# One transformer block on one core: the late rows' norm and operands behind the up products of the third to sixth feed-forward groups, stored from the norm weight's tile

## The chip, the cores and the metric

The kernel runs on one core of a Trainium2 chip (trn2). The metric is device time in microseconds (us) of one execution, and the time of a kernel is the median over its runs. The five engines are named as in the profile: PE (TensorE), DVE (VectorE), ACT (ScalarE), POOL (GpSimd) and SP (SyncE, which here only issues DMAs). Each engine executes its instructions in a fixed order, which a scheduler writes down when the kernel is built. An instruction that has to wait therefore holds up everything behind it on its engine.

## The reference

One layer of width 1024 over 2048 rows (`S` = 2048, `D` = 1024, f32 in and out):

```python
u    = rms_norm(h, norm1_w[l])
proj = u @ w_in[l]                  # split into q, k, v of two kinds of heads
y    = concat(diff_attention(...), stick_breaking_attention(...))
h    = h + y @ w_out[l]
u2   = rms_norm(h, norm2_w[l])
gate = u2 @ w_gate[l]               # 1024 x 2816
up   = u2 @ w_up[l]                 # 1024 x 2816
h    = h + (silu(gate) * up) @ w_down[l]
```

The change lies in the last four lines, the feed-forward part.

## The kernel before

**Products.** Every f32 operand is held as two fp16 halves (high and low), and one product of two f32 blocks is three fp16 matmuls. The feed-forward products use one level of Strassen-Winograd: instead of eight block products, `quad` does seven, each 12 matmuls of 128x512 (`product`). For that, rows and weights are first mixed into seven operands; those of the rows are called X and lie in DRAM as `xcd[half]`.

**Steps.** The feed-forward part is 22 steps: two halves of 1024 rows, and in each half 11 groups of 256 columns (`NFG` = 11), `(half, fg)` in `steps`. A step is a gate quad (columns of `w_gate`), in some steps the down products of two groups that are finished (`down`, with 168 matmuls, in steps 2, 4, 6 and so on), and an up quad (columns of `w_up`). Counting from 0, step 2 works on the third group. Between the seven products of a quad stand hooks: `in_gate(1..7)` and `in_up(1..7)`; `row(s)` is called in each, with s = 1 to 7 in the gate quad and 8 to 14 in the up quad.

**Weights.** In the first half the hooks also drive `load_ffn` for the weights of the next group. For each of the three matrices a tile is fetched into one of two `stages` buffers (L925 for gate and up, L923 for down), ACT squares it into `sq`, which has one buffer (L954 for gate and up, L190 for down), PE forms the column sums `fsc` (L963), DVE makes scales of them (L964 and some small ones), and ACT and DVE write the scaled high and low halves (L216, L221) into the weight tile `wg`, `wu` or `wd`, while POOL mixes blocks (L98). The tile is also stored to `split` (L919), from where the second half reads it again. Three such chains follow one another in each step, since `sq` is one buffer, and PE executes the `fsc` matmuls in its fixed order.

**Quads.** The sums of the seven products are formed on DVE as they come: L1047, L1052, L1057, L1067, L1071. The tiles `cg` (gate) and `cu` (up) hold them; L1083 is the silu on ACT, L1103 the product of up and gate, L1097 and L98 make the fp16 operand `act` of the down products. PE writes the products into tiles of PSUM (`pa`, `pm`, `pd`), and a product that needs a used tile waits for DVE or ACT to have read it.

**Down.** `down` adds its products to the rows' residual: for each pair of row tiles, `load_hs` loads two tiles from DRAM (L1128) into the tag `hs`, which has four buffers, DVE adds (L1144), and the tiles are stored again (L1187). A load into a buffer waits until the store from it has landed.

**The late rows.** Rows 12 to 15 of the second half's 16 row tiles come too late from the attention part to be normed there. `build_x` does this for them in two pairs, j = 2 and 3. It takes all four `hs` buffers: `w2f` for the norm weight spread over 128 partitions, `xa` and `xb` for the pair's row tiles, and `xt`. It is a generator, and each call of `tick` runs it to its next `yield`: load (L1203), norm (`norm_tile`: ACT square L226, small scale L155, DVE product L229), 16 transposes on PE (L1213) with copies back on ACT (L1214), and then in `x_ops` four times `put`: a cast to fp16 on ACT (L89), a subtraction for the low half on POOL or DVE (L98), a store to `xcd[1]` (L238); between the puts stand four subtractions of operands (L98). The fp16 operands are formed in slices of `b16`, a tile with the tag `wd` used as three buffers. The operands are first read when the second half begins, in step 11 (`load_x(1, XL)`).

Where the ticks stand is in `late_at`: in steps 0 and 1, at the hooks listed there, and one tick ahead of step 0. The fetch of the second group's `w_up` is held until the second row tile's load is issued (`issue_after(rows[1].ins)`).

## Time and profile before

| | us |
|---|---|
| median of 3 runs | 2679.68 |
| lowest and highest run | 2678.3, 2680.41 |
| profiled execution, its own time | 2682.59 |
| span of the profiled execution | 2680.8 |
| PE busy in the span | 2492.4 (93%) |
| feed-forward steps 0 to 5 in the span | about 1427 to 1757 |

The profile records one execution. In a timeline a row gives the start, the busy time, the engine, the line, the operation with what it writes and reads, and how many instructions in a row it stands for; in square brackets stand the idle time of the engine just ahead, and what ended it. A row of several matmuls is pipelined: its busy time includes the tail of the last one, and the next row starts a little ahead of its end. In the steps considered here a product of 12 matmuls takes 2.75 us in a row of its own, and one follows the other every 2.59 us.

### The profile page before, as it was taken

To read this page: it belongs to the slowest core of one execution; us is meant where nothing else is said; L and a number is where in the kernel's file an instruction comes from. 1 tells how busy PE (TensorE), PEld (TensorE's weight loads), DVE (VectorE), ACT (ScalarE), POOL (GpSimd) and SP (SyncE) were. 2 spreads that over 40 slices of the span, in tenths; PEclk is the share of its full clock that TensorE was granted. 3 is DMA by queue.
4 is the path that set the end of the run, shared out by engine and by line. 5 is a ranking of instruction groups with operands and counts; after the bars stand their busy time and mean duration, and the time that the engine had idled before them with its cause. 6 is when DMAs were issued, how large, how long until landed. Compare 5 with 4: busy or idle time off the path is not lost. (4 is left out here: it accounts for less than half of the span.)

```text
span 2680.8 us, 50579 instructions
## 1 busy us (share of the span) xinstructions
PE 2492.4 (93%) x19628; PEld 1498.6 (56%) x19628; DVE 1932.7 (72%) x3711; ACT 1347.0 (50%) x2487; POOL 1489.1 (56%) x1098
## 2 busy tenths in 40 slices
PE   6998989888988989889989899999999999999999
PEld 4655656577776776557775344444444444444444
DVE  6898969898989989877766868777685544444434
ACT  4665656567978878665644535344352112111121
POOL 2578667667767766546764656565564232322323
PEclk9999999999999999999999899999999999999999
DMA  6777697767998979987897574665649743635532
GB/s 222 213 162 181 146 200 168 179 143 184 193 179 179 185 160 209 210 191 217 218 285 282 208 250 178 255 226 202 245 183 346 293 177 143 233 141 186 195 111 95
DMA packets 619585, 534.41 MB, mean 199 GB/s; under 512 B 480640, under 2 KB 548224, under 8 KB 609104
## 3 DMA queue, kind: packets, MB, share of 16 engines
q1 hardware_dynamic: 617520, 529.09, 69.9%
q8 instruction: 154, 2.52, 0.4%
q0 software_dynamic: 512, 1.36, 0.2%
q14 instruction: 87, 0.71, 0.1%
q10 hardware_dynamic: 1312, 0.72, 0.1%
HBM read 261.08 MB, written 147.32 MB: 152 GB/s over the span
## 5 line engine op out<-in xcount | busy, mean ns | idle before, releaser
L98 POOL TENSOR_TENSOR s<-z,s 128x1024 f16<-128x1024 f32 (+7 forms) x288 | 472.0, 1647 | 142.5 <-ACT s L89 109.8
L507 PE MATMUL sc<-kT,qT 128*128 128x512 f16 (+3 forms) x1520 | 382.0, 353 | 53.3 <-DVE z L623 19.3
L622 DVE TENSOR_TENSOR_SCAN z<-z,sc 128x512 f32<-128x512 f32 (+3 forms) x320 | 352.8, 1112 | 58.6 <-ACT sc L620 38.0
L1138 PE MATMUL pd<-wd,act 128*128 128x512 f16 x1764 | 390.9, 379 | 1.2 <-DVE cg L1071 1.2
L326 PE MATMUL pj<-w,xt 128*128 128x384 f16 x1920 | 352.2, 331 | 18.8 <-ACT xt L683 6.9
L1030 PEld LDWEIGHTS <-wg 128*128 128x128 f16 x1848 | 182.0, 99 | 230.2 <-issue 16.4
L518 PE MATMUL yp<-v,aT 128*128 128x64 f16 (+1 forms) x4896 | 269.8, 204 | 41.6 <-DMA aT<-s 40.2
L518 PEld LDWEIGHTS <-aT 128*128 128x128 f16 x4896 | 237.5, 99 | 120.4 <-DMA aT<-s 52.5
L1030 PEld LDWEIGHTS <-wu 128*128 128x128 f16 x1848 | 180.7, 98 | 218.0 <-issue 2.6
L98 POOL TENSOR_TENSOR act<-cg,act 128x512 f16<-128x512 f32 x112 | 148.5, 1337 | 262.9 <-ACT act L1097 150.8
L1138 PEld LDWEIGHTS <-act 128*128 128x128 f16 x1764 | 172.8, 98 | 209.4 <-issue 2.8
L326 PEld LDWEIGHTS <-xt 128*128 128x128 f16 x1920 | 187.3, 99 | 147.5 <-issue 21.4
L89 ACT CAST s<-z 128x128 f16<-128x128 f32 (+7 forms) x215 | 173.1, 809 | 134.1 <-DMA aT<-s 40.5
L98 POOL TENSOR_TENSOR hs<-hs,cu 128x512 f32<-128x512 f32 x99 | 130.9, 1328 | 171.3 <-DVE hs L1144 70.8
L619 ACT ACTIVATE z<-sc,c 128x512 f32<-128x512 f32 (+3 forms) x320 | 210.7, 663 | 25.6 <-PE sc L507 11.7
L1097 ACT CAST act<-cg 128x512 f16<-128x512 f32 x126 | 77.3, 616 | 238.4 <-DVE cg L1103 162.7
L507 PEld LDWEIGHTS <-qT 128*128 128x128 f16 x1520 | 128.4, 99 | 121.0 <-DVE z L623 23.0
L832 PE MATMUL po<-wo,mt 128*128 128x256 f16 x1536 | 180.7, 277 | 13.9 <-DVE xf L835 8.4
L1030 PE MATMUL pm<-X,wu 128*128 128x512 f16 x792 | 180.4, 379 | 1.3 <-DVE wu L221 1.3
L1030 PE MATMUL pm<-X,wg 128*128 128x512 f16 x792 | 181.3, 382 | 0.0
L342 PE MATMUL pj<-xt,w 128*128 128x128 f16 x2304 | 175.0, 220 | 6.7 <-DVE v L364 5.7
L1144 DVE SCALAR_TENSOR_TENSOR hs<-pd,c,hs 128x512 f32<-128x512 f32 x136 | 99.0, 747 | 109.6 <-PE pd L1138 83.1
(266 smaller groups left out, 4737.6 us busy)
## 6 DMA issues: line engine op xcount, KB each, us to landing
xt<-xs SPq DMA_DIRECT2D x112, 512.0 KB, 4.3
hs<-hd SPq DMA_DIRECT2D x68, 512.0 KB, 4.5
hd<-hs SPq DMA_DIRECT2D x56, 512.0 KB, 4.7
split<-wg SPq DMA_DIRECT2D x11, 1792.0 KB, 7.8
split<-wu SPq DMA_DIRECT2D x11, 1792.0 KB, 6.7
split<-wd SPq DMA_DIRECT2D x11, 1792.0 KB, 7.2
wg<-split SPq DMA_DIRECT2D x11, 1792.0 KB, 7.3
wd<-split SPq DMA_DIRECT2D x11, 1792.0 KB, 12.2
```

The source lines that it names most:

```text
L89: ACT.copy(dst, src)
L98: (DVE if e == "D" else POOL).tensor_tensor(dst, a_, b_, op)
L326: PE.matmul(pj[:, :384], lhsT=xv[:, xi, kt, :], rhs=G["w"][:, wi, kt, :], start=n == 0, stop=n == 23)
L342: PE.matmul(o, lhsT=x_ if c == 2 else w_, rhs=w_ if c == 2 else x_, start=n == 0, stop=n == 23)
L507: last = PE.matmul(sc[:, : 128 * w].rearrange("p (t n) -> p t n", n=P), lhsT=G["q"][i // 4][:, a_, i % 4, :], rhs=G["k"][q][:, b_, 0:w, :] ...
L518: PE.matmul(yp[:, y0 : y0 + wd], lhsT=aT[:, a_, :], rhs=v[:, v_ : v_ + wd], start=start and j == 0 and q == 0, stop=stop and j == nb - 1 a ...
L619: ACT.activation(om[:, lo:hi], sc[:, :w], AF.Sigmoid, scale=G["nkz"][:])
L622: DVE.tensor_tensor_scan(ov, ov, sc[:, :w], om[:, hi : hi + 1], op0=ALU.mult, op1=ALU.bypass)
L832: PE.matmul(po[:, sl], lhsT=mt[:, kt, P * xi : P * xi + P], rhs=wos[2 * h + n][wi][:, kt, :], start=q == 0, stop=q == 23)
L1030: front[0] = PE.matmul(ps_[:].rearrange("p (t n) -> p t n", n=P), lhsT=wv[:, wo, wi, 128 * kt : 128 * kt + 128], rhs=X[xo][:, :, xi, kt, : ...
L1138: front[0] = PE.matmul(po[:], lhsT=act[:, ao, xi, 128 * j : 128 * j + 128], rhs=W["d"][:, wo, wi, :], start=start and u == 0 and q == 0, s ...
L1144: DVE.scalar_tensor_tensor(dst, po[:], kd[:], src, op0=ALU.mult, op1=ALU.add)
```

## The change

Line numbers behind the first edits are lower by 2, later by up to 8; L1198 is the scaling of the norm weight (L1192 before), L1195 the row loads (L1203), L1196 the load of the norm weight (L1191), L1207 and L1208 the transposes and their copies (L1213, L1214).

- The ticks move from steps 0 and 1 to steps 2 and 3 (pair j = 2) and 4 and 5 (pair j = 3). In steps 2 and 4 they stand at hooks 9, 11, 12 and 13, all in the up quad, behind the down products; in steps 3 and 5 at hooks 7, 8, 9, 11 and 12.
- The four `hs` tiles are taken anew for each pair. The norm weight is loaded for each pair, behind the pair's two row tiles, and scaled for each pair.
- The fp16 operands are formed in the bytes of `w2f`, as one buffer in place of the three in `b16`. Each put's cast thus waits for the store of the put ahead.
- The norms of the two tiles stand in ticks of their own.
- The fetch of the second group's `w_up` isn't held any longer.

```diff
             def stage(fg, nme):
...
-                with tc.issue_after(rows[1].ins) if (fg, nme) == (1, "u") else nullcontext():
-                    fetch(st, f0, nme)
+                fetch(st, f0, nme)
...
             def build_x():
-                w2f, xa, xb, xt = (hp.tile([P, D], F32, tag="hs", bufs=4, name=nm("bx")) for _ in range(4))
-                SP.dma_start(w2f[:], a["norm2_w"].partition_broadcast(P))
-                DVE.tensor_scalar(w2f[:], w2f[:], r_24[:], None, op0=ALU.mult)
-                b16 = fd.tile([P, 7, 2, 512], F16, tag="wd", bufs=2, name=nm("b16"))[:].rearrange("p o s n -> p (o s n)")
-                n = [0]
-
                 def bufs():
-                    n[0] = (n[0] + 1) % 3
-                    return b16[:, 2048 * n[0] : 2048 * n[0] + 2048]
+                    return w2f[:].bitcast(F16)
 
                 d2 = lambda z: z[:].rearrange("p (d n) -> p d n", d=2)
                 for j in (2, 3):
+                    w2f, xa, xb, xt = (hp.tile([P, D], F32, tag="hs", bufs=4, name=nm("bx")) for _ in range(4))
                     for q, z in enumerate((xa, xb)):
-                        rows.append(SP.dma_start(z[:], hd[8 + 2 * j + q]))
+                        SP.dma_start(z[:], hd[8 + 2 * j + q])
+                    SP.dma_start(w2f[:], a["norm2_w"].partition_broadcast(P))
                     yield
+                    DVE.tensor_scalar(w2f[:], w2f[:], r_24[:], None, op0=ALU.mult)
                     for z in (xa, xb):
                         norm_tile(z[:], z[:], w2f[:], xt[:])
-                    yield
+                        yield
                     for z in (xa, xb):
...
                     yield from x_ops([d2(z) for z in (xa, xb)], d2(xt), 1, j, bufs, "AP", "DP")
+                    yield
...
-            tick(1)
             load_now(0, 0, "d", W)
...
-            late_at = ((5, 9, 10, 11, 12, 13, 14), (3, 7, 8, 9, 10, 11, 12))
+            late_at = {2: (9, 11, 12, 13), 3: (7, 8, 9, 11, 12), 4: (9, 11, 12, 13), 5: (7, 8, 9, 11, 12)}
...
-                    if i < 2 and s in late_at[i]:
+                    if s in late_at.get(i, ()):
                         tick(1)
```

What this does to the engines' orders is seen at three places. The first is DVE in the up quad of step 2. The rows of before: the last additions of the down products, the three sums of the up quad, and the maximum that belongs to the down weight's scale.

```order
L1144 SCALAR_TENSOR_TENSOR hs_23436<-pd_23548,c_23099,hs_23436 128x512
L1144 SCALAR_TENSOR_TENSOR hs_23435<-pd_23527,c_23099,hs_23435 128x512
L1047 TENSOR_TENSOR cu_23575<-pm_23579,cu_23575 128x512
L1052 TENSOR_TENSOR cu_23614<-pm_23601,cu_23575 128x512
L1057 TENSOR_TENSOR cu_23637<-pd_23624,cu_23614 128x512
L184 TENSOR_REDUCE m_23644<-fsc_23643 128x1
```

The same place of the change; `bx_23486` is `w2f`, `bx_23487` and `bx_23488` are `xa` and `xb`, and `xrs` is the small scale of a row's norm.

```order
L1142 SCALAR_TENSOR_TENSOR hs_23320<-pd_23412,c_22984,hs_23320 128x512
L1045 TENSOR_TENSOR cu_23460<-pm_23464,cu_23460 128x512
L155 TENSOR_SCALAR xrs_23548<-xss_23546 128x1
L1198 TENSOR_SCALAR bx_23486<-bx_23486,c_17372 128x1024
L1050 TENSOR_TENSOR cu_23506<-pm_23493,cu_23460 128x512
L155 TENSOR_SCALAR xrs_23575<-xss_23573 128x1
L229 SCALAR_TENSOR_TENSOR bx_23487<-bx_23487,xrs_23548,bx_23486 128x1024
L229 SCALAR_TENSOR_TENSOR bx_23488<-bx_23488,xrs_23575,bx_23486 128x1024
L1055 TENSOR_TENSOR cu_23529<-pd_23516,cu_23506 128x512
L184 TENSOR_REDUCE m_23536<-fsc_23535 128x1
```

The scaling of the norm weight and both norms now stand between the first and the third sum of the up quad; none of them was here before. On PE, the pair's 16 transposes (L1207) now stand in the same quad, between its sixth product (`pm_23579`) and its seventh, which adds to `pd_23516` after L1055 has read it.

The second place is SP behind the down products of step 2. Before, the stores of the rows (L1187) alternate with the loads for the next down (L1128):

```order
L1187 DMA hd<-hs_23365 128x1024
L1128 DMA hs_24071<-hd 128x1024
L1187 DMA hd<-hs_23364 128x1024
L1128 DMA hs_24072<-hd 128x1024
L1187 DMA hd<-hs_23436 128x1024
L1187 DMA hd<-hs_23435 128x1024
L1128 DMA hs_24235<-hd 128x1024
L1128 DMA hs_24236<-hd 128x1024
L925 DMA stages<-in_w_gate_dram 128x8x256
```

In the change the two row tiles and the norm weight take the places of these loads:

```order
L1185 DMA hd<-hs_23250 128x1024
L1195 DMA bx_23487<-hd 128x1024
L1185 DMA hd<-hs_23249 128x1024
L1195 DMA bx_23488<-hd 128x1024
L1185 DMA hd<-hs_23321 128x1024
L1185 DMA hd<-hs_23320 128x1024
L1196 DMA bx_23486<-in_norm_w_dram 128x1024
L923 DMA stages<-in_w_gate_dram 128x8x256
L917 DMA split<-wd_23534 128x7168
L238 DMA xcd_87<-bx_23486 128x2x1024 x2
L1126 DMA hs_24016<-hd 128x1024
L921 DMA stages<-in_w_down_dram 128x2x1024
```

The load of the norm weight is now the last one behind all the stores, ahead of the next `w_gate` fetch; the loads for the next down come behind the stores of the first operands.

The third place is ACT in step 3 of the change. L89 is the cast of a put, L216 and L952 belong to the weights of the next group (`sq_23788` is the square of the next `w_gate` tile).

```order
L89 CAST bx_23486<-bx_23488 128x2x512
L216 ACTIVATE wu_23693<-stages,c_23659 128x2x512 x2
L216 ACTIVATE wu_23693<-sx_23710,c_23659 128x512
L1081 ACTIVATE cg_23745<-cg_23745,c_23482 128x512
L1081 ACTIVATE cg_23762<-pa_23662,c_23482 128x512
L216 ACTIVATE wu_23693<-sq_23660,c_23659 128x2x512
L89 CAST bx_23486<-bx_23489 128x2x512
L952 ACTIVATE sq_23788<-stages 128x2048
```

The casts of the second and the third put, each of which writes into `w2f`, now stand ahead of the weights' work of this step; before, no cast of the late rows stood in step 3.

More of the change, by code (lines that the diff above doesn't have):

```diff
@@ L894, in block @@
             scales = {}
-            rows = []
             front = [None]
```

## The prediction

> **What bounds the kernel now.** First the page's line of busy times, then a table of stretches of 60 us, to see where in the feed-forward part PE is not full. Its columns are the stretch, its length, busy time (and count) of PE, PEld, DVE, ACT, POOL, the granted clock of PE, the DMA share and GB/s.
>
> ```profile
> PE 2492.4 (93%) x19628; PEld 1498.6 (56%) x19628; DVE 1932.7 (72%) x3711; ACT 1347.0 (50%) x2487; POOL 1489.1 (56%) x1098
> ...
> 1460.00:1520.00 60.00, 52.53 (x250) 25.11 (x249) 50.62 (x61) 32.21 (x42) 42.56 (x26) 0.94 0.61 226
> 1520.00:1580.00 60.00, 52.92 (x240) 24.19 (x238) 44.56 (x70) 26.00 (x31) 37.53 (x27) 0.94 0.68 237
> 1580.00:1640.00 60.00, 60.00 (x289) 28.40 (x288) 42.27 (x67) 26.74 (x32) 29.06 (x21) 1.00 0.63 223
> ...
> 1700.00:1760.00 60.00, 59.34 (x286) 27.89 (x284) 46.92 (x75) 31.88 (x38) 30.41 (x22) 1.00 0.59 214
> ```
>
> PE is the bound, but not everywhere. In steps 0 to 2, where the late rows are now (up to 1520) and just behind them, PE lacks 7 us in each stretch and its clock is 0.94. From step 2's up quad to step 3 (1580 to 1640) and in step 5 (1700 to 1760), where they are to go, PE is full at clock 1.00, with DVE at 42 to 47 us. So the change takes work from where PE waits and puts it where it doesn't.
>
> Next, PE's timeline: every gap of steps 0 to 2.
>
> ```profile
> 1443.88 2.76 PE L1030 MATMUL pd<-X,wg 128*128 128x512 f16 x12 [0.96 <-DMA X<-xcd]
> ...
> 1466.50 2.75 PE L1030 MATMUL pd<-X,wu 128*128 128x512 f16 x12 [1.36 <-DVE cu L1057]
> ...
> 1491.13 4.76 PE L1030 MATMUL pd<-X,wg 128*128 128x512 f16 x12 [5.47 <-DVE cg L1057]
> ...
> 1517.50 2.75 PE L1030 MATMUL pd<-X,wu 128*128 128x512 f16 x12 [0.64 <-DVE cu L1057]
> ...
> 1533.90 1.87 PE L963 MATMUL fsc<-sq,ones 128*128 128x256 bf16 x8 [5.88 <-ACT sq L954]
> 1535.56 7.34 PE L1030 MATMUL pm<-X,wg 128*128 128x512 f16 x24
> ...
> 1547.98 1.46 PE L1138 MATMUL pd<-wd,act 128*128 128x512 f16 x6 [1.19 <-DVE cg L1071]
> 1549.37 1.03 PE L963 MATMUL fsc<-sq,ones 128*128 128x256 bf16 x8
> ```
>
> The longest but one is DVE's doing. Its own rows ahead of L1057:
>
> ```profile
> 1484.25 2.17 DVE L229 SCALAR_TENSOR_TENSOR bx<-bx,xrs,bx 128x1024 f32<-128x1024 f32 x1
> 1486.34 3.48 DVE L221 SCALAR_TENSOR_TENSOR wu<-stages,c,wu 128x1024 f16<-128x1024 f32 x2
> ...
> 1490.40 0.68 DVE L1057 TENSOR_TENSOR cg<-pd,cg 128x512 f32<-128x512 f32 x1
> ```
>
> A norm of the late rows (2.17) and the weight split behind it hold L1057, and PE with it.
>
> **What leaves steps 0 to 2.** From 1443 to 1534 the stalls are 0.96 + 1.36 + 5.47 + 0.64 + 5.88 = 14.31 us. After the 5.47 the 12 matmuls took 4.76 for the usual 2.75: 2.01 more at a lowered clock, in all 16.3. I let all of it go. The 5.88 ends on the square of the next gate weight, which stands on ACT behind the down weight; that weight's tile has the tag of `b16`, whose stores are gone. The 1.19 and the slow clock behind the 5.88 (7.34 for 24 matmuls) I keep: between the two `fsc` rows at 1533.90 and 1549.37 lie 15.5 us, and that is a weight chain by itself. One undisturbed, in step 3:
>
> ```profile
> 1608.52 1.04 PE L963 MATMUL fsc<-sq,ones 128*128 128x256 bf16 x8
> ...
> 1623.86 1.04 PE L963 MATMUL fsc<-sq,ones 128*128 128x256 bf16 x8
> ```
>
> ```profile
> 1620.94 1.91 ACT L954 ACTIVATE sq<-stages 128x2048 bf16<-128x2048 f32 x1 [0.61 <-DVE wu L221]
> ```
>
> From the `fsc` to the end of the next square are 1622.85 − 1608.52 = 14.3 us, so two `fsc` can't follow much closer. That is also why a gap closed may come back: bounds of the gain are 16.3, and 5.5 if only the L1057 and L1057-like stalls of DVE (5.47) go and the rest is met again by the chain. I take 16.3, since step 3's chains, with no late rows beside them, leave PE no gap.
>
> At this place a rule can be weighed. The clock after the 5.47 gap was lowered (4.76 for 2.75). The Trainium skill, "TensorE: Matmul & The Clock Gate", Part 1: The HAM clock gate, has PE fall to half its clock after an idle window of about 3.4 us and come back after as long a busy one; by that rule a full window of 12 matmuls at half clock would cost an estimated 2.6 us, the trace's row says 2.0, and the sum goes by 2.0.
>
> **What moves without a price.** The late rows' work itself, from the view of that tile (min/median/max in ns, all counts of both pairs):
>
> ```profile
> L89 ACT CAST b<-bx x8: 618/1045/1069, 1456.2 to 1509.6; 128x1024 f16<-128x1024 f32 x6, 128x512 f16<-128x512 f32 x2
> ...
> L229 DVE SCALAR_TENSOR_TENSOR bx<-bx,xrs,bx x4: 1906/2160/2284, 1448.8 to 1491.0; 128x1024 f32<-128x1024 f32 x4
> L98 POOL TENSOR_TENSOR b<-bx,b x3: 2367/3108/3118, 1459.7 to 1512.4; 128x1024 f16<-128x1024 f32 x3
> L98 POOL TENSOR_TENSOR bx<-bx,bx x3: 2132/2157/2249, 1469.7 to 1507.4; 128x512 f32<-128x512 f32 x3
> ...
> L1192 DVE TENSOR_SCALAR bx<-bx,c x1: 752/752/752, 1445.3 to 1445.3; 128x1024 f32<-128x1024 f32 x1
> ```
>
> ```profile
> 1452.53 1.04 PE L1213 MATMUL xtr<-id,bx 128*128 128x128 f32 x8
> ```
>
> The transposes are on PE before and after: 1.04 us for eight, with a tail that the next row covers, so 2.05 for a pair's 16 at most. One more scaling (0.75) and one more load of 512 KB are added, whose places are below.
>
> **What it costs in steps 2 and 3.** SP's rows at the end of step 2's down:
>
> ```profile
> 1590.09 0.32 SPq L1128 DMA_DIRECT2D hs<-hd  x1
> 1590.50 0.86 SPq L1187 DMA_DIRECT2D hd<-hs  x2
> 1595.72 1.54 SPq L1128 DMA_DIRECT2D hs<-hd  x2
> ```
>
> ```profile
> hs<-hd SPq DMA_DIRECT2D x3, 512.0 KB, 4.4
> hd<-hs SPq DMA_DIRECT2D x2, 512.0 KB, 5.6
> ```
>
> Each load follows the landing of a store (the last two rows are the DMA issues from 1588 to 1597, with the median us to landing). The last load, at 1595.72, becomes the norm weight's. By the 4.4 it lands at 1600.1. The square of the first tile writes `xt`, in the buffer of the last store, and can't start ahead of 1596 either. On DVE, L155 and L1198 then wait directly behind the first sum of the up quad:
>
> ```profile
> 1589.36 0.69 DVE L1047 TENSOR_TENSOR cu<-pm,cu 128x512 f32<-128x512 f32 x1 [1.84 <-PE pm L1030]
> ```
>
> Queued behind them are the second and third sum, both norms and the down weight's maximum, and PE waits for these: its transposes need the norms, its seventh product the third sum.
>
> ```profile
> 1599.67 2.75 PE L1030 MATMUL pd<-X,wu 128*128 128x512 f16 x12
> ```
>
> So DVE stands from 1590 to 1600.1; then 0.75 + 0.69 + 2 x 2.16 make 1605.9. PE is at its transposes at 1599.67, does the first eight (1.04) behind the first norm, waits, and has done all at about 1607: 5.4 us of stall beside the 2.05 of transposes, and as after the 5.47 gap 2.0 of slow clock.
>
> Three more rows are needed: the page's landing of the operands' stores, the stretch at the start of step 3 (columns as above), and a DVE row in it.
>
> ```profile
> xcd<-b SPq DMA_DIRECT2D x6, 512.0 KB, 5.8
> ```
>
> ```profile
> 1595.00:1612.50 17.50, 17.50 (x87) 8.31 (x86) 17.01 (x27) 9.90 (x13) 8.46 (x6) 1.00 0.69 252
> ```
>
> ```profile
> 1605.91 1.75 DVE L1103 SCALAR_TENSOR_TENSOR cg<-cu,c,cg 128x512 f32<-128x512 f32 x1
> ```
>
> Behind that the puts run one at a time, as all four write into `w2f`: cast 1.05, subtraction 3.1, issue 0.4, landing (5.8) make 10.35 each. With the first cast at 1608.5, the third is at 1629.2; POOL's own operand subtractions (2.16 and 3.1) stand between, to about 1635.6. The square of the next gate weight stands behind that cast on ACT (1.91), so its `fsc`, at 1623.86 before, comes at 1637.6: 13.7, less the 2.05 that the transposes only move, is **11.7**. DVE has little room there (17.01 of 17.50 us are busy). Its rows are also stretched while POOL subtracts: L1103 took 1.75 us here, L1047 on the same size 0.69 above. Operand subtractions that fall to DVE and one or two such stretches of 1.0 I put at 1.8, an estimate: 13.5.
>
> At this stretch a second rule can be weighed. The Trainium skill, "SBUF — State Buffer", section SBUF: two separate sides, has VectorE and GpSimd share a pair of ports that one instruction locks for its whole length. That speaks against the change: a subtraction of 3.1 put beside a full DVE could hold it for its full length, not for 1.0, and by it each pair would lose an estimated 3 us more; the sum takes the 1.8.
>
> **What it costs in steps 4 and 5.** The same, with less wait for the loads:
>
> ```profile
> 1704.48 0.40 SPq L1187 DMA_DIRECT2D hd<-hs  x1
> 1705.78 6.97 SPq L1128 DMA_DIRECT2D hs<-hd  x2
> ```
>
> The second of the last two loads is issued behind 1712, so the store at 1704.48 landed 7.9 us after its issue; the square waits for it, and L155 starts at about 1713.6. From there stand on DVE L1198 and L1103 (0.75 each), the two norms (4.3), and between these the rest of the down weight's split and two sums (some 4 us, an estimate from the 3.48 + 0.68 of L221 and L1057 above): the second norm ends at 1723.6. PE would begin its transposes at 1714.98:
>
> ```profile
> 1714.98 2.75 PE L1030 MATMUL pa<-X,wg 128*128 128x512 f16 x12
> ...
> 1737.41 1.04 PE L963 MATMUL fsc<-sq,ones 128*128 128x256 bf16 x8
> ```
>
> That is 7.6 us, and 2.0 of slow clock. The `fsc` at 1737.41 comes at 1748.2: 10.8, less 2.05 for the transposes, is **8.7**; with the same stretch 10.5. The steps behind I let stand as they are.
>
> **The sum.** −16.3 + 11.7 + 8.7 = +4.1 without the stretch, −16.3 + 13.5 + 10.5 = +7.7 with it; I take the middle, +5.9. The profiled execution's own time is 2682.59 (1.8 around its span), 2.9 above the median of the runs; it becomes 2688.5, and the median 2679.7 + 5.9 = **2685.6**.
>
> **Rivals.** (1) Faster: DVE isn't held. That is so if the norm weight has landed and the first square is done when DVE gets to L1198 (by 1590 in the terms above), and if the chain of puts is hidden behind step 3's products. Price: the stalls and slow clocks (5.4 + 2.0 and 7.6 + 2.0) go, of each pair only its scaling and norms on a full DVE stay (0.75 + 2 x 2.16 = 5.1), the sum is −16.3 + 10.2 = −6.1, 2673.6. For it: the down loads before it land within 4.4. Against: the load waits for a store's landing, and the 1595.72 is in the trace. It decides from a load issued ahead of about 1586 (4.4 ahead of 1590). (2) The gain fails: the weight chain is the bound of steps 0 to 2, and only 5.5 go; −5.5 + 20.4 to 24.0 = +14.9 to +18.5, 2696.4 in the middle. For it: every second gap ends on that chain; against: step 3 has no gap. (3) The norm weight's load takes as long as the one in the trace:
>
> ```profile
> bx<-in_norm_w_dram SPq DMA_DIRECT2D x1, 512.0 KB, 10.0
> ```
>
> That is 5.6 more for pair one; for pair two 1705.8 + 10.0 = 1715.8 for the 1713.6 above, 2.2 more: 2693.4. Against: beside that load four others started. (4) Gains and losses meet, and nothing is measured, or the work stands in other places than the steps suppose: within 0.2%.
>
> **How the numbers follow.** Within 0.2% (5.4 us) is what a measurement of this kernel can hardly tell from no change. Forecast 0.42, of its own range 2680 to 2692, which lies on both sides of that bound: 0.27 slower, 0.15 same. Rival 1: 0.2, of it 0.18 faster. Rival 2: 0.13, rival 3: 0.15, both slower. Rival 4: 0.10. In sum slower 0.55, same 0.27, faster 0.18. The range reaches from rival 1 to rival 2 and a little over: 2672 to 2698; left out are the gain of 16.3 with no loss (2663) and rivals 2 and 3 together (2704).
>
> **What would show it.** In the profile after: no gap over 2 us on PE in steps 0 and 1, and the one on `sq` L954 in step 2 gone; then a gap of some 5 us ahead of L1207 in step 2's up quad and of 7 in step 4's, both ended by DVE `bx` L229, with DVE's own idle ended by the norm weight's DMA or `xrs`; and a gap ahead of L963 in steps 3 and 5 ended by ACT `sq` L952. The forecast is wrong if DVE's L1198 doesn't wait, or if L963 in steps 3 and 5 isn't late by about 10 us.

## The result, and the profile after

The changed kernel takes 2690.65 us (median of 5 runs, 2687.61 to 2695.94), the kernel before 2679.68 (5 runs, 2677.7 to 2684.17). The ratio is 1.0039, with a 95% interval of 1.0027 to 1.0052: slower by 10.5 us (7.2 to 13.9). The forecast was 2685.6, slower by 5.9.

The profiled execution has a span of 2694.1 us, 13.3 longer than before, and 3.2 of these lie ahead of the feed-forward part, where both kernels do the same work. In the profiled executions of this study the first gate product starts anywhere from 1417.9 to 1430.4 us. So traces are compared from that product on: 1253.58 us to the end of the span before, 1263.73 after, +10.15, which is what the runs say. The stretches of 60 us show where (columns as in the prediction; the start is 3.2 us later than before).

```profile
1460.00:1520.00 60.00, 60.00 (x293) 28.54 (x292) 47.82 (x69) 31.64 (x38) 36.97 (x27) 1.00 0.50 191
1520.00:1580.00 60.00, 56.42 (x266) 26.00 (x265) 34.53 (x51) 18.19 (x22) 32.02 (x24) 1.00 0.63 225
1580.00:1640.00 60.00, 49.98 (x233) 23.44 (x231) 52.22 (x83) 34.47 (x45) 36.24 (x23) 0.94 0.56 204
...
1700.00:1760.00 60.00, 51.51 (x234) 24.54 (x233) 45.40 (x66) 31.23 (x40) 30.75 (x19) 0.91 0.56 198
```

The picture of before is turned round: PE is full from 1460 to 1520 and lacks 8 to 10 us, at a lowered clock, in the two stretches that were full. PE's timeline of the changed kernel from the end of step 2 to step 5 has these gaps, shown with the later sums of each gate quad:

```profile
1584.51 1.09 PE L1207 MATMUL xtr<-id,bx 128*128 128x128 f32 x8 [2.72 <-DVE bx L229]
1586.34 1.06 PE L1207 MATMUL xtr<-id,bx 128*128 128x128 f32 x8 [0.73 <-DVE bx L229]
...
1598.39 1.03 PE L961 MATMUL fsc<-sq,ones 128*128 128x256 bf16 x8 [0.84 <-ACT sq L952]
...
1611.74 5.28 PE L1028 MATMUL pd<-X,wg 128*128 128x512 f16 x12 [4.34 <-DVE cg L1055]
...
1621.38 1.03 PE L961 MATMUL fsc<-sq,ones 128*128 128x256 bf16 x8 [1.39 <-ACT sq L952]
...
1718.33 1.97 PE L1207 MATMUL xtr<-id,bx 128*128 128x128 f32 x8 [3.99 <-DVE bx L229]
1720.09 4.43 PE L1028 MATMUL pa<-X,wg 128*128 128x512 f16 x12
...
1742.83 4.22 PE L1028 MATMUL pd<-X,wg 128*128 128x512 f16 x12 [3.21 <-DVE cg L1055]
...
1749.26 1.04 PE L961 MATMUL fsc<-sq,ones 128*128 128x256 bf16 x8
```

There are two kinds: at the transposes, which wait for the norms, and ahead of the fourth gate product, which waits for the third sum. After the longer ones the clock is low (5.28, 4.43 and 4.22 us for 12 matmuls that take 2.75). The first kind in DVE's timeline:

```profile
1571.32 0.69 DVE L1045 TENSOR_TENSOR cu<-pm,cu 128x512 f32<-128x512 f32 x1 [1.84 <-PE pm L1028]
1580.51 0.15 DVE L155 TENSOR_SCALAR xrs<-xss 128x1 f32<-128x1 f32 x1 [8.50 <-ACT bx L226]
1581.85 0.76 DVE L1198 TENSOR_SCALAR bx<-bx,c 128x1024 f32<-128x1024 f32 x1 [1.19 <-DMA bx<-in_norm_w_dram]
```

DVE stands for 8.50 us behind the first sum, as foreseen. The square on ACT ends this wait, and 1.19 more goes to the norm weight, which comes last. The square in turn waits for a store, the one from the buffer that `xt` takes over (ACT's timeline):

```profile
1579.33 1.06 ACT L226 ACTIVATE bx<-bx 128x1024 f32<-128x1024 f32 x1 [11.32 <-DMA hd<-hs]
```

The second kind is in DVE's timeline, in step 3's gate quad, ahead of the L1055 that PE waits for:

```profile
1596.60 2.17 DVE L98 TENSOR_TENSOR bx<-bx 128x512 f32<-128x512 f32 x1
1598.69 1.75 DVE L98 TENSOR_TENSOR act<-cg,act 128x512 f16<-128x512 f32 x1
1600.36 1.75 DVE L1101 SCALAR_TENSOR_TENSOR cg<-cu,c,cg 128x512 f32<-128x512 f32 x1
...
1609.44 1.65 DVE L98 TENSOR_TENSOR bx<-bx,bx 128x1024 f16<-128x1024 f32 x1
1611.01 0.68 DVE L1055 TENSOR_TENSOR cg<-pd,cg 128x512 f32<-128x512 f32 x1
```

Behind 1590.48 no row up to 1611.01 has idle time ahead of it. Late-row subtractions stand between the sums; those that DVE does ahead of 1611.01 take 5.2 us (2.17, 1.65 and two of 0.68). The kernel's own rows beside them take up to 1.75 (L1101 takes 0.74 to 0.75 a few rows earlier) while POOL mixes the next weight, as it did before (L1103 with 1.75 in the prediction):

```profile
1598.17 1.73 POOL L98 TENSOR_TENSOR sx<-stages 128x512 f32<-128x512 f32 x1
1599.97 1.59 POOL L98 TENSOR_TENSOR stages<-stages 128x512 f32<-128x512 f32 x1
```

The L1101 at 1600.36 ends at 1602.1, 0.55 behind the end of POOL's second row. The Trainium skill, "SBUF — State Buffer", section SBUF: two separate sides, has an instruction of VectorE with two inputs in SBUF and one of GpSimd that reads SBUF keep each other out, whichever starts first, until its end. By that rule L1101 begins its work at about 1601.6; the 0.55 that is left is 0.2 short of the 0.74 that it takes alone, so the trace agrees roughly.

In step 5 it is the kernel's own weight split that holds L1055, with a late-row subtraction on POOL beside it. DVE's rows, then POOL's:

```profile
1737.34 4.83 DVE L221 SCALAR_TENSOR_TENSOR wu<-stages,c,wu 128x1024 f16<-128x1024 f32 x2 [1.27 <-ACT wu L216]
1742.10 0.68 DVE L1055 TENSOR_TENSOR cg<-pd,cg 128x512 f32<-128x512 f32 x1
```

```profile
1737.98 3.11 POOL L98 TENSOR_TENSOR bx<-bx,bx 128x1024 f16<-128x1024 f32 x1
```

One such L221 took 1.27 at 1713.12; here two take 4.83.

**A ruler.** The column sums of the gate and up weights (`fsc<-sq`, eight matmuls, L963 before) stand at about the same places of the steps in every kernel and mark off what a stretch of PE's timeline lasts. Numbered from step 0, the fifth is at the start of step 2's down (1549.37 before), the sixth and seventh at the two ends of step 3's gate quad (1608.52, 1623.86), the ninth in step 4's down (1668.99), the tenth and eleventh in step 5 (1721.24, 1737.41), the thirteenth in step 6's down (1780.78). The table gives the distances between their starts in each kernel's profiled execution, beside the feed-forward part as a whole and the ratio of the runs. Where a stretch holds the same instructions in the same order it repeats to 0.1 us (101.0 and 59.2).

| kernel | feed-forward | to sum 5 | 5-6 | 6-7 | 7-9 | 9-10 | 10-11 | 11-13 | runs against before (95%) |
|---|---|---|---|---|---|---|---|---|---|
| before | 1253.6 | 122.2 | 59.2 | 15.3 | 45.1 | 52.3 | 16.2 | 43.4 | |
| change | 1263.7 | 101.0 | 67.1 | 23.0 | 44.7 | 62.6 | 20.6 | 44.9 | 1.0039 (1.0027 to 1.0052) |
| e1 no late rows | 1231.4 | 100.9 | 59.2 | 15.3 | 44.7 | 51.6 | 16.6 | 43.2 | 0.9912 (0.9897 to 0.9928) |
| e2 pair one | 1249.5 | 101.0 | 66.3 | 23.0 | 46.4 | 52.7 | 16.2 | 44.6 | 0.9973 (0.9962 to 0.9983) |
| e3 pair two | 1246.5 | 101.0 | 59.2 | 15.3 | 44.7 | 61.4 | 21.0 | 44.4 | 0.9962 (0.9949 to 0.9974) |
| e4 old place | 1258.3 | 125.7 | 60.5 | 15.3 | 45.1 | 52.2 | 16.2 | 43.4 | 1.0016 (1.0003 to 1.0028) |
| e5 POOL | 1269.7 | 101.0 | 65.5 | 25.9 | 48.9 | 59.5 | 23.6 | 45.5 | 1.0067 (1.0051 to 1.0082) |
| e6 halves | 1265.4 | 101.0 | 65.6 | 23.7 | 46.8 | 60.3 | 23.1 | 45.1 | 1.0044 (1.0028 to 1.0060) |
| e7 later norms | 1258.4 | 101.0 | 59.2 | 22.7 | 46.7 | 56.6 | 26.4 | 45.3 | 1.0015 (1.0004 to 1.0026) |
| e8 one each | 1252.7 | 112.8 | 59.2 | 22.3 | 46.2 | 52.4 | 16.6 | 43.2 | 0.9997 (0.9986 to 1.0008) |
| e9 no subtractions | 1248.3 | 100.9 | 68.8 | 14.8 | 44.7 | 61.9 | 13.8 | 43.4 | 0.9987 (0.9975 to 1.0000) |
| e10 steps 6, 7 | 1250.6 | 100.9 | 59.2 | 22.7 | 46.8 | 52.8 | 16.2 | 43.2 | 0.9988 (0.9975 to 1.0002) |
| e11 up quad | 1254.0 | 100.9 | 59.2 | 16.4 | 54.5 | 52.7 | 16.2 | 43.2 | 1.0007 (0.9998 to 1.0016) |
| e12 norms apart | 1259.8 | 101.0 | 62.2 | 21.4 | 48.2 | 51.8 | 16.2 | 43.4 | 1.0030 (1.0015 to 1.0045) |

The difference of the feed-forward column from before, and that of the runs (ratio times 2680), agree within 3.2 us in every row, so the table may be read as the time to that extent.

The scheduler doesn't always put a sum behind the same matmul, and then two neighbouring stretches trade matmuls of 0.216 us each (2.59 for 12). Between sums 5 and 6 the change has 275 of them for 269 before, and between 6 and 7 it has 61 for 67. So of the 7.9 us by which 5-6 grows, 1.3 come from 6-7. The next table takes these matmuls out, and the 2.05 of the pair's transposes where they stand; what is left is PE time lost against before.

| kernel | matmuls in 5-6 and 6-7 | lost in 5-6 | lost in 6-7 |
|---|---|---|---|
| before, e1 | 269, 67 | 0 | 0 |
| change | 275, 61 | 4.6 | 8.9 |
| e2 pair one | 275, 61 | 3.8 | 9.0 |
| e5 POOL | 275, 61 | 3.0 | 11.9 |
| e6 halves | 276, 60 | 2.9 | 9.9 |
| e7 later norms | 269, 67 | 0.0 | 5.4 |
| e9 no subtractions | 275, 61 | 6.3 | 0.8 |
| e12 norms apart | 283, 53 | 0.0 | 7.0 |

In the same way 9-10 has 242 matmuls in the change for 237 before, and 10-11 has 64 for 67: 7.2 us are lost ahead of step 5's gate quad and 5.1 in it.

### The profile page after: what moved, and what is told of

Read it like the earlier page. It is cut to its first block, busy times and chain, and to the rows that moved or that the text cites. A ratio compares the mean times of both kernels' runs of the same rounds, so it can differ in the third digit from the quotient of the medians.

```text
span 2694.1 us, 50591 instructions
## 1 busy us (share of the span) xinstructions
PE 2506.2 (93%) x19628; PEld 1504.2 (56%) x19628; DVE 1935.0 (72%) x3713; ACT 1346.8 (50%) x2488; POOL 1485.1 (55%) x1096
## 3 DMA queue, kind: packets, MB, share of 16 engines
q8 instruction: 154, 2.52, 0.4%
## 5 line engine op out<-in xcount | busy, mean ns | idle before, releaser
L326 PE MATMUL pj<-w,xt 128*128 128x384 f16 x1920 | 358.6, 335 | 14.7 <-ACT raw L375 5.8
L89 ACT CAST s<-z 128x128 f16<-128x128 f32 (+7 forms) x215 | 173.2, 810 | 137.9 <-DMA aT<-s 46.4
## 6 DMA issues: line engine op xcount, KB each, us to landing
wd<-split SPq DMA_DIRECT2D x11, 1792.0 KB, 11.7
```

The costliest lines, as they stand in the source:

```text
L89: ACT.copy(dst, src)
L326: PE.matmul(pj[:, :384], lhsT=xv[:, xi, kt, :], rhs=G["w"][:, wi, kt, :], start=n == 0, stop=n == 23)
```

## The experiments

### What a pair costs, in each place: e1 to e4

e1 leaves the late rows out: no tick runs, and the second half reads the first half's operands for pairs 2 and 3. e2 and e3 leave one pair out in the same way. The edit of e1:

```diff
-            late_at = {2: (9, 11, 12, 13), 3: (7, 8, 9, 11, 12), 4: (9, 11, 12, 13), 5: (7, 8, 9, 11, 12)}
+            late_at = {}
...
-                    SP.dma_start(X[o][:].rearrange("p t s k n -> p (t s k n)"), xcd[half][o].rearrange("p t n -> p (t n)"))
+                    for src, j0, j1 in (((1, 0, 2), (0, 2, 4)) if half else ((0, 0, 4),)):
+                        SP.dma_start(X[o][:, j0:j1].rearrange("p t s k n -> p (t s k n)"), xcd[src][o][:, j0:j1].rearrange("p t n -> p (t n)"))
```

> The late rows are left out altogether: no load, norm, transpose or operand of row tiles 12 to 15; the second half's first groups read the first half's operands in their place, over the same bytes. What is left is the steps without them, so that both kernels can be held against it. Theory 1 (place): before the change the late rows cost PE about 17 us of stalls and slow clock in steps 0 to 2 and 4.1 us of transposes; the time is about 2679.7 - 21 = 2659. Theory 2 (chain): the weights' chains bound steps 0 to 2 anyway, and without the late rows only 5.5 us of stalls and the 4.1 go: about 2670.

Measured: 0.9912, 23.6 us less than before. The part up to the fifth sum takes 100.9 us for 122.2, 21.2 less. Theory 1 holds: what the late rows cost there goes with them, 4.1 of transposes by the prediction's count and so 17.1 of waits and slow clock. The weights' chains bound these steps only between sums 4 and 5, where e1 keeps gaps of 1.96 and 1.61. The change gets all of the 21.2 (101.0).

> The changed kernel with pair j = 2 alone, in steps 2 and 3; pair j = 3 is left out, its operands are the first half's. Theory 1: pair one costs what the trace shows between the column sums of step 2 and of step 4, 12.6 us beside 2.05 us of transposes, so 14.7 above e1. If the two pairs' losses are independent, this and the next add up to the changed kernel. Theory 2 (a pair's cost comes from what both hold together, such as the second load of the norm weight or the row loads pushed back): clearly less than 14.7, and the sum of both falls short of the changed kernel by 5 us or more.

> The changed kernel with pair j = 3 alone, in steps 4 and 5; pair j = 2 is left out. Theory 1: 13.1 us between the column sums of step 4 and of step 5, 2.05 us of transposes and 1.5 us in step 6, so 15 to 17 above e1. Theory 2: clearly less, the rest only when both are there.

Measured: e2 lies 18.1 us above e1 in the feed-forward part, e3 15.1; by the runs 16.4 and 13.4. 18.1 + 15.1 = 33.2 for the 32.3 by which the change lies above e1, so by the traces the two pairs are independent. By the runs they add up to 29.8 for 34.0; that is 4.2 short, less than the 5 that theory 2 asked for, and each ratio is known only to some 3 us. Neither pair costs clearly less than theory 1 said, so theory 2 falls, though the runs alone wouldn't exclude a few us of it. Of e2's 18.1, 14.8 lie between sums 5 and 7, as in the change. Of the rest, 1.7 lie between 7 and 9 (24 matmuls take 6.77 for 5.34 behind a gap of 2.63 ahead of sum 7), 1.1 between 9 and 10, where five more matmuls stand than in e1, and 1.4 in step 6, where e2 has no late rows: there the product behind a gap of 3.31, which is 3.30 before, takes 5.28 for 4.13.

e4 puts the changed code back to the old place:

```diff
+            tick(1)
             load_now(0, 0, "d", W)
...
-            late_at = {2: (9, 11, 12, 13), 3: (7, 8, 9, 11, 12), 4: (9, 11, 12, 13), 5: (7, 8, 9, 11, 12)}
+            late_at = {0: (5, 6, 9, 10, 11, 12, 13, 14), 1: (1, 3, 4, 7, 8, 9, 10, 11, 12)}
```

> The changed code (norm weight loaded per pair, operands formed in its tile one at a time, norms in ticks of their own) at the ticks of before: steps 0 and 1. Theory 1 (place): the loss of the change is that of steps 2 to 5, so this is near the kernel before; the 5.9 us stall on the square in step 2 should go since no weight buffer is taken, the puts that wait for one another may give some of it back: 2672 to 2682. Theory 3 (form): the waits of the casts for the stores in one tile are what costs, and they cost here as well: 2685 to 2695.

Measured: 1.0016, +4.3 us; 1258.3 in the feed-forward part. That is between the two expectations. In the old place the form of the change, with the three more ticks that it needs, costs 4.7 us (1258.3 for 1253.6). The stall of 5.88 ahead of the fourth sum is gone, as theory 1 had it, but PE has others in its place: 4.97 ahead of transposes, 3.68 and 2.52 ahead of fourth gate products and 3.04 for a load of X, in all 17.8 us of gaps up to the fifth sum for 15.5 before. With the same code the pairs cost 26.9 us in steps 0 and 1 (1258.3 for e1's 1231.4) and 32.3 where they now are. So of the change's 10.2, 4.7 go with the form, as far as its price in the old place tells, and 5.4 with the place.

### The gate quad: puts or subtractions? e5, e6, e9

The prediction had the stretch behind the norms grow because puts wait for one another in one tile, so that ACT's square stands behind a cast. The rival is that DVE and POOL have no room for the subtractions. e5 moves all of them to POOL, e6 removes the wait between puts.

```diff
-                    yield from x_ops([d2(z) for z in (xa, xb)], d2(xt), 1, j, bufs, "AP", "DP")
+                    yield from x_ops([d2(z) for z in (xa, xb)], d2(xt), 1, j, bufs, "AP", "P")
```

> The changed kernel with all subtractions of the late rows on POOL (before, POOL or DVE by load). Theory 1 (DVE is full in the gate quad of steps 3 and 5): DVE gets 5.2 us of each pair back between its 1595 and 1612, L1055 comes earlier and PE's gaps of 4.34 and 3.21 ahead of the fourth gate product shrink to under 2, with their slow clock: 6 to 10 us less than the changed kernel, so 0 to +5 against before. Theory 2 (the puts wait for one another in one tile): each subtraction gets longer (2.6 to 3.1 on POOL for 1.65 on DVE), the third cast and the square behind it come later: +10 to +16 against before.

Measured: 1.0067, +18.0 us, beyond even theory 2's range and not for its reason. PE's gaps and POOL's and ACT's rows in step 3's gate quad:

```profile
1605.66 2.75 PE L1028 MATMUL pd<-X,wg 128*128 128x512 f16 x12 [2.11 <-DVE cg L1055]
...
1620.47 1.87 PE L961 MATMUL fsc<-sq,ones 128*128 128x256 bf16 x8 [9.47 <-ACT sq L952]
```

```profile
1608.66 2.24 POOL L98 TENSOR_TENSOR sq<-stages 128x512 f32<-128x512 f32 x1
1610.87 3.79 POOL L98 TENSOR_TENSOR bx<-bx,bx 128x1024 f16<-128x1024 f32 x2
1614.62 1.25 POOL L98 TENSOR_TENSOR sq<-stages,sq 128x512 f32<-128x512 f32 x1
```

```profile
1615.90 1.15 ACT L216 ACTIVATE wu<-sq,c 128x1024 f16<-128x1024 f32 x1 [3.10 <-POOL sq L98]
```

The gap ahead of the fourth gate product goes from 4.34 to 2.11 and loses its slow clock, as theory 1 says of DVE. But the subtractions now stand between the two halves of the weight's mixing on POOL (3.79 between two rows on `sq`), ACT splits the mixed weight late, the next square and its column sum come late: 9.47. The weight's chain runs through DVE and POOL both, and a subtraction lengthens it on either.

And e6, where the puts at 2 and 4 are halved in the same way as this one:

```diff
+                turns = [0]
+
                 def bufs():
-                    return w2f[:].bitcast(F16)
+                    turns[0] ^= 1024
+                    return w2f[:].bitcast(F16)[:, turns[0] : turns[0] + 1024]
...
+            def puts(o, src):
+                for d in range(2) if half and j > 1 else ():
+                    put(o + d, src[:, d : d + 1])
+                if not (half and j > 1):
+                    put(o, src)
...
...
-            put(0, xn[0])
+            puts(0, xn[0])
```

> The changed kernel with each put of two operands split in two of one, which take turns in two halves of the norm weight's tile, so that a cast no longer waits for the store just ahead (seven stores of 256 KB for four of 512). Theory 2 (puts wait for one another): ACT isn't held by the casts, the square behind the third put comes earlier, 5 us or more less than the changed kernel: 0 to +6 against before. Theory 1 (DVE is full): casts and stores were off the path, and more instructions are added: +8 to +14 against before.

Measured: 1.0044, +11.8 us, against +10.5 for the change: no gain, and 23.7 us between sums 6 and 7 as against 23.0. Since e6 also adds casts, subtractions and stores, a small gain could hide behind their cost. The change's own ACT rows in step 3 settle it there: the third put's cast follows without idle time, and the square behind it waits for DVE, not for a store.

```profile
1616.44 1.15 ACT L216 ACTIVATE wu<-sq,c 128x1024 f16<-128x1024 f32 x1 [2.91 <-POOL sq L98]
1617.50 1.03 ACT L89 CAST bx<-bx 128x1024 f16<-128x1024 f32 x1
1619.41 1.91 ACT L952 ACTIVATE sq<-stages 128x2048 bf16<-128x2048 f32 x1 [0.89 <-DVE wu L221]
```

So in step 3 the waits of puts for one another cost nothing.

e9 takes the late rows' subtractions away and leaves everything else; the low halves are copies, and the mixed operands are not formed:

```diff
-                tt(xv[:, :, 1, :], src, xv[:, :, 0, :], ALU.subtract, 512 * k, tte)
+                if half and j > 1:
+                    ACT.copy(xv[:, :, 1, :], xv[:, :, 0, :])
+                else:
+                    tt(xv[:, :, 1, :], src, xv[:, :, 0, :], ALU.subtract, 512 * k, tte)
...
-            tt(xt[:, 1], xn[1][:, 1], xn[1][:, 0], ALU.subtract, 512, tte)
... (and three more)
+            if not (half and j > 1):
+                tt(xt[:, 1], xn[1][:, 1], xn[1][:, 0], ALU.subtract, 512, tte)
... (and three more)
```

> The changed kernel without the late rows' subtractions: the mixed operands aren't formed, and the low half of each put is a copy of the high one, made on ACT (1 us each). Loads, norms, transposes, casts and stores stay, each put still waits for the store ahead. Theory 1 (the subtractions on DVE and POOL, in the middle of the weights' chain of steps 3 and 5, lengthen that chain): the stretch between the two column sums of step 3 goes back from 23.0 us to 16 to 17, that of step 5 from 20.6 to 16 to 17, and with their gaps and slow clocks 9 to 13 us go: -2 to +2 against before. Theory 2 (ACT is held by casts that wait for stores): these stay, and ACT gets more to do, +8 to +14 against before.

Measured: 0.9987, 13.9 us less than the change by the ratios, 15.4 in the feed-forward part: a little more than theory 1 had. The column sum at the end of step 3's gate quad no longer waits long, 14.8 us behind the one before (PE's timeline of e9):

```profile
1611.62 1.03 PE L965 MATMUL fsc<-sq,ones 128*128 128x256 bf16 x8 [0.60 <-ACT sq L956]
```

Step 5's stretch is 13.8 us. Both hold six or seven matmuls fewer than before, so they are not shorter than without late rows; but only 0.8 us are lost in step 3's, for the change's 8.9, and nothing in step 5's. The casts and stores are all in place, with more on ACT. The stretches ahead (68.8 and 61.9) stay long: that is the hold. So the two losses are separate, and the subtractions are the second. Whether by the work that they add on DVE, by the order on POOL or by rows that lengthen side by side isn't told apart; e9 takes all of these away at once.

### The hold: e7, e12

e7 keeps the loads where they are and holds the scaling and the norms on DVE behind the last sum of the up quad, the transposes behind them:

```diff
+                    with tc.issue_after(dl[0]):
+                        DVE.tensor_scalar(w2f[:], w2f[:], r_24[:], None, op0=ALU.mult)
                     for z in (xa, xb):
-                        norm_tile(z[:], z[:], w2f[:], xt[:])
+                        with tc.issue_after(dl[0]):
+                            norm_tile(z[:], z[:], w2f[:], xt[:])
...
-            late_at = {2: (9, 11, 12, 13), 3: (7, 8, 9, 11, 12), 4: (9, 11, 12, 13), 5: (7, 8, 9, 11, 12)}
+            late_at = {2: (9,), 3: (1, 2, 3, 5, 7, 8, 10, 12), 4: (9,), 5: (1, 2, 3, 5, 7, 8, 10, 12)}
```

(`dl[0]` is the last sum that `quad` has issued on DVE.)

> The changed kernel with the scaling and the norms held on DVE behind the last sum of the up quad of steps 2 and 4, and the transposes behind them, in the gate quad of steps 3 and 5; loads as in the change. Theory 3 (hold: DVE stands for the square and the norm weight ahead of the sums that PE needs): PE's gaps at the transposes go (2.72 + 0.73 in pair one; 0.62 + 3.99 and some 2.6 of slow clock in pair two), 8 to 11 us less than the changed kernel: 0 to +3 against before. Theory 1 (DVE is full): the norms fall into the full stretch, and the gaps ahead of the fourth gate product grow by as much: +8 to +14 against before.

Measured: 1.0015, +4.0 us, 6.4 less than the change, just above theory 3's range and far below theory 1's. The stretch of step 2 is 59.2 again: the hold is gone there, to the tenth of a microsecond. In step 4 it is 56.6 for 62.6. Of what was expected to go, a part comes back: the transposes still wait for norms on a busy DVE, and step 5's gate quad is longer (26.4 for 20.6; of that 2.05 are the transposes, which now stand there, and 1.7 eight more matmuls). PE's timeline of e7 in step 3:

```profile
1582.83 1.09 PE L1210 MATMUL xtr<-id,bx 128*128 128x128 f32 x8 [1.62 <-DVE bx L229]
...
1587.81 1.21 PE L1210 MATMUL xtr<-id,bx 128*128 128x128 f32 x8 [1.95 <-DVE bx L229]
```

e12 sets the two norms apart, the first behind the third sum of the up quad, the second behind the first sum of the next gate quad, in steps 2 and 3, and 6 and 7 (the edit against e7):

```diff
-            late_at = {2: (9,), 3: (1, 2, 3, 5, 7, 8, 10, 12), 4: (9,), 5: (1, 2, 3, 5, 7, 8, 10, 12)}
+            late_at = {2: (9, 11), 3: (2, 4, 6, 7, 8, 10, 12), 6: (9, 11), 7: (2, 4, 6, 7, 8, 10, 12)}
```

> The pairs in steps 2 and 3, and 6 and 7; the first norm held behind the third sum of the up quad, the second behind the first sum of the gate quad of the next step, the transposes behind its fourth product. In the run with both norms behind the up quad the transposes waited 1.54 + 1.94 us in pair one and 0.37 + 3.33 in pair two. If these gaps are the rest of the hold, they go and nothing takes their place: 5 to 8 us less than that run, -12 to -6 against before. Rival (DVE and POOL are full in the chain, and the same work waits elsewhere): -5 to +1 against before.

Measured: 1.0030, +8.0 us: worse than either side expected. DVE now gets to the scaling ahead of the norm weight:

```profile
1570.93 0.75 DVE L1200 TENSOR_SCALAR bx<-bx,c 128x1024 f32<-128x1024 f32 x1 [3.51 <-DMA bx<-in_norm_w_dram]
```

That wait holds nobody up: PE runs without a gap to the end of the up quad, and the 62.2 between sums 5 and 6 are 14 more matmuls. What is lost, 7.0 us, is lost in the gate quad, where PE waits 1.70 at the second transposes, 1.41 ahead of a product and 3.65 for the square (PE's timeline of e12):

```profile
1605.11 1.86 PE L962 MATMUL fsc<-sq,ones 128*128 128x256 bf16 x8 [3.65 <-ACT sq L953]
```

So the rival had the kind right and the size too low. Moving the work about within these steps moves the wait.

### Other places: e8, e10, e11

e8 leaves pair one in steps 0 and 1, spread wider, and has pair two in steps 2 and 3; e10 is e7 with its second pair in steps 6 and 7; e11 has the norms behind the gate quad of steps 3 and 7, the puts in halves in their up quads.

```diff
+            late_at = {0: (5, 9, 13), 1: (3, 6, 8, 10, 12), 2: (9,), 3: (1, 2, 3, 5, 7, 8, 10, 12)}   # e8, with a tick(1) ahead of step 0
+            late_at = {2: (9,), 3: (1, 2, 3, 5, 7, 8, 10, 12), 6: (9,), 7: (1, 2, 3, 5, 7, 8, 10, 12)}   # e10
+            late_at = {2: (9,), 3: (6, 7, 8, 9, 10, 11, 12, 13), 6: (9,), 7: (6, 7, 8, 9, 10, 11, 12, 13)}   # e11
```

> Pair one in the old place, spread over steps 0 and 1, pair two as in the run with late norms in steps 2 and 3; steps 4 and 5 free. If each place has some slack that one pair can use (both pairs in steps 0 and 1 cost 23.6 us, one pair in steps 2 and 3 about 16.4), half of the old cost or less and less than 14 of the new: 18 to 24 above the kernel without late rows, so -5 to 0 against before. If the first pair disturbs the weights' chains as both did, +5 or more.

Measured: 0.9997, no difference from before and within the first expectation's -5 to 0. One pair alone in steps 0 and 1 costs 11.9 us (112.8 for 100.9), about half of what both cost there (21.2 by the trace, 23.6 by the runs), so the first pair isn't free in this place either; pair two costs 8.5 in steps 2 and 3.

> The run with later norms, its second pair in steps 6 and 7 in place of 4 and 5. In the trace of that run the first pair costs 9.4 us (with its transposes) and the second 16.9; the stretch from the down weight's column sum of step 4 to step 5 is shorter (51.6 us without late rows) than that of step 2 (59.2). Theory 4 (the second pair is dearer because of its steps): in steps 6 and 7, with a stretch of 59.1, it costs 9 to 12: -5 to -1 against before. Rival (it is dearer because it is the second pair, with later loads): 15 to 18 as in steps 4 and 5, +2 to +6 against before.

Measured: 0.9988 (0.9975 to 1.0002), 3.2 us less than before; 2.9 by the feed-forward part. The second pair costs 8.6 us in steps 6 and 7 (the three stretches there are 59.2, 24.1 and 44.9, and 59.2, 15.2 and 45.1 without late rows) as against 16.9 in steps 4 and 5 in e7. Theory 4 holds: the second pair is dear because of its steps. Of the kernels that do the whole work it is the fastest here, though its interval still takes in no change.

> The late rows further back: loads behind the down of steps 2 and 6, norms and transposes held behind the gate quad's sums of steps 3 and 7, the puts in halves in their up quads, where the column sums stand 30 us apart for 15 in the gate quad. Theory 1 (what costs is work inside the 15 us chain): the chain keeps its 15 us, a pair costs its transposes and some 3 us: -12 to -5 against before. Rival (the puts run into the next gate quad and delay the loads for the next down): one or two waits of 5 us there, -2 to +6.

Measured: 1.0007, +1.9 us, as the rival had it. The gate quad keeps its chain (16.4 us), but the up quad and the next gate quad take 54.5 for 44.7: the work isn't hidden there either.

## Why the prediction was right, and where not

**The gain of steps 0 to 2** was put at 16.3. It is 17.1 (21.2 less the 4.1 of transposes, e1 and the change alike). Letting all the stalls go was right; rival 2, that the chain would keep them, is refuted by e1. What I had kept didn't stay as it was: the slow clock behind the 5.88 went too, and in place of the 1.19 stand the 1.95 and 1.63 that e1 has as well.

**Pair one** was put at 11.7 to 13.5. It is 13.1: stretches 5 to 9 take 134.8 for 119.6, less 2.05. The size was right, and its first half was right in kind: DVE stands behind L1045 for the square and the norm weight, 9.7 us for the 10.1 foreseen, and holds PE (e7 takes it away: 59.2). But the stall at the transposes was 3.45, for 5.4 foreseen, and had no slow clock behind it, since norms took 1.28 each here in place of 2.16. Ahead of the gate quad 7.4 were foreseen and 4.6 lost, by the table that takes the matmuls out.

**The puts** are the step that failed in kind: "the puts run one at a time ... The square of the next gate weight stands behind that cast". No cast of step 3 waited for a store (in step 5 one did, for 2.53, behind the square of the next gate weight), halving the puts gained nothing (e6), and the subtractions, on a DVE and a POOL with no room for them, are the cause (e9: 0.8 us lost in the gate quad for 8.9; e5: 11.9). I had the puts at 4.3 in the gate quad (11.7 less 7.4), and at 1.8 beside them the subtractions on DVE with the stretched rows; but all of the 8.9 except 0.8 went with the subtractions. That pair one came out right is luck: 2.8 too much ahead of the gate quad, and 2.8 to 4.6 too little in it. The 3 us more for each pair that the prediction estimated and left out of its sum would have been nearer.

**Pair two** is the term that was mis-sized: 8.7 to 10.5 foreseen, 14.2 measured (128.1 for 111.8, less 2.05). The prediction's own terms don't add up there: 7.6 + 2.0 + 2.05 put the sum of 1737.41 at 1749.1 and not at 1748.2. Ahead of the gate quad, 7.2 for the 7.6 + 2.0 foreseen. In the gate quad 5.1 were lost, where I had nothing but the 1.8 of the stretch, though the puts and their subtractions stand in it. And with "The steps behind I let stand" I missed 1.5 in step 6, whose gap grew from 3.30 to 3.81 and whose product took 5.28 us for 4.13. The latter is hardly pair two's: e2, which has no pair two, loses as much there behind a gap of 3.31.

The sum by the trace, without transposes: −17.1 + 13.1 + 14.2 = +10.2, for the −16.3 + 12.6 + 9.6 of the prediction's middle. Of the 4.3 between 10.2 and 5.9, pair two makes 4.6 and pair one 0.5, and the gain takes 0.8 back. Rival 3, a slow load of the norm weight, didn't come: in pair one SP issued it at 1577.89, and DVE went on with it at 1581.85, 4.0 us later. Rival 1 is refuted by DVE's 8.50. Of the signs, those on steps 0 and 1 and on the gaps at the transposes came, with 2.72 + 0.73 for some 5 and 0.62 + 3.99 for 7. The gap ahead of the sum of L961 came with 1.39 in step 3 and not at all in step 5; the sums are late all the same, since PE stands at the fourth gate product instead.

Why the second pair in steps 4 and 5 still costs 16.9 us where the norms are later (e7), when steps 6 and 7 take it for 8.6, can be read from e7's trace in part. ACT, DVE and PE, each from its own timeline:

```profile
1692.48 1.06 ACT L226 ACTIVATE bx<-bx 128x1024 f32<-128x1024 f32 x1 [12.79 <-DMA hd<-hs]
...
1702.13 1.91 ACT L953 ACTIVATE sq<-stages 128x2048 bf16<-128x2048 f32 x1 [1.48 <-DVE wd L221]
```

```profile
1696.26 1.28 DVE L221 SCALAR_TENSOR_TENSOR wd<-stages,c,wd 128x1024 f16<-128x1024 f32 x1 [6.46 <-ACT wd L216]
```

```profile
1704.09 1.37 PE L962 MATMUL fsc<-sq,ones 128*128 128x256 bf16 x8 [4.72 <-ACT sq L953]
```

The squares of the late rows wait on ACT for a store, and the split of the down weight stands behind them; DVE waits for that split, the next gate weight's square for DVE, and PE for the square. In e10 PE has no gap between the same two sums of steps 6 and 7. These 4.72 us and their slow clock are over half of the difference. No run takes this wait away by itself, so its share stays a reading.

## What to carry to other kernels

Before work is moved to a place where the bottleneck engine is full, look at the engines that feed it there: a stretch in which PE has no gap and DVE is busy 17 of 17.5 us has no room, while the old place with its visible gaps may be no dearer. Where a chain of small steps over several engines repeats at nearly the pace of its own length (14.3 us here, for 15.3 between sums), work put on the engines of the chain lengthens it (8.9 us of PE here, in a gate quad where DVE alone had 5.2 us of it), and moving it to the neighbour engine moved the gap (e5). When two traces are compared by markers, count what stands between the markers: a scheduler may have moved some of it across. Taking the work out altogether (e1) and leaving one kind of it out (e9) told what it costs and why, which no rearrangement did by itself.

## What the runs showed of the hardware

The clock after a gap isn't set by the gap's length alone. In step 6 eight of the kernels have the same 24 matmuls, then 3.29 to 3.31 us of idle, then the 12 matmuls of the fourth gate product. These took 2.75 us in e11, 4.09 in e9, 4.13 before, 4.26 in e10, 4.44 in e4 and e12 and 5.28 in e2 and e3. PE's timelines of e11, of the kernel before and of e2:

```profile
1762.38 2.75 PE L1035 MATMUL pd<-X,wg 128*128 128x512 f16 x12 [3.31 <-DVE cg L1062]
```

```profile
1773.91 4.13 PE L1030 MATMUL pd<-X,wg 128*128 128x512 f16 x12 [3.30 <-DVE cg L1057]
```

```profile
1767.26 5.28 PE L1028 MATMUL pd<-X,wg 128*128 128x512 f16 x12 [3.31 <-DVE cg L1055]
```

Shorter gaps were charged too: 12 matmuls took 4.39 us behind 2.52 of idle in e4 and 4.01 behind 2.13 in e11. The Trainium skill, "TensorE: Matmul & The Clock Gate", Part 1: The HAM clock gate, says that the window by which idle time is judged runs freely. That fits one gap with prices from 0 to 2.5 us, though no run here moves the window by itself. The idle window of about 3.4 us that it gives doesn't fit the shorter gaps, and the measurement decides.

And the parts of a program that repeat in the profile to 0.1 us (the stretches above) stand beside a part, here the attention ahead of them, whose end moves by 12 us between the profiled executions of these kernels; a difference of 10 us is better read from the former.
